# Joining the delta rule's inverse from diagonal 64-wide blocks, each in its own quarter of the TensorE array

## The chip, the core and the metric

The kernel runs on one core of a Trainium2 chip. The metric is device time in microseconds (us) of one execution. The work is two layers of a hybrid trunk (Hyena long convolution, gated delta rule, latent attention, mixture of experts) over 256 latent and 256 context tokens, in one program for all five engines.

## The reference, cut to what matters

The change lies in the gated delta rule. For each chunk of 64 tokens, head and direction the reference solves a unit lower triangular system of 64 rows and applies the inverse to the values and keys:

```python
C = GDN_CHUNK                                   # 64
gamma = jnp.exp(jnp.where(causal, gc[..., :, None] - gc[..., None, :], -jnp.inf))
kb = kc * bc[..., None]
m = jnp.where(strict, jnp.einsum('nbhid,nbhjd->nbhij', kb, kc) * gamma, 0.0)
eye = jnp.eye(C, dtype=F32)
t_inv = lax.linalg.triangular_solve(eye + m, jnp.broadcast_to(eye, m.shape), left_side=True, lower=True, unit_diagonal=True)
u = t_inv @ (vc * bc[..., None])
w = t_inv @ (kb * jnp.exp(gc)[..., None])
```

Then a scan over the chunks carries a 128 x 128 state per head and direction. It is done for context and latent tokens, 4 heads, both directions, in each of 2 layers.

## The kernel before, in words

The kernel works on chunks of 128 tokens in place of the reference's 64, so its inverse is one of 128 x 128 matrices. `gdn_pair` (L930) runs once per layer and pair of heads: it makes the features, then calls `gdn_system` (L1044) twice, for `base` 2 (the context) and `base` 0 (the latent tokens), and runs `gdn_scan` (L1202) for each. So there are 2 layers x 2 pairs x 2 bases = 8 systems. A system holds 8 matrices (2 directions, 2 chunks, 2 heads), four side by side in one tile of 128 x 512 for each direction `d`.

Inside a system, VectorE first inverts the diagonal 16-wide blocks by elimination (the loop over `j`, 15 steps of small operations; its rows are the ones that read `rsel` products). T holds the inverses and U their transposes. Then the blocks are joined: 16 to 32 wide, 32 to 64 wide (the two inner steps, the loop over `n` at L1148), and 64 to 128 wide (a step of its own behind it, already in 64 x 64 pieces). One inner step does, for each direction: N.U, four matmuls of 128 x 128 into one PSUM bank; `copy_predicated` on VectorE, which takes the wanted blocks of the bank into V (V starts as the identity); then T.V and V.T, four matmuls each into two banks, and two copies on ScalarE back into U and T. That is 3 bank products x 2 directions x 2 steps = 12 bank products a system, 96 in the program. Matrices that are block diagonal with blocks of 64 stay so until the last step.

The matmuls are in 32-bit floats; each of them is two MATMUL records in the trace (rows called `128*128 128x128 f32` are rows x columns of the stationary operand, then the shape that streams). The large projections are instead three matmuls on operands split into high and low parts, one record each (`128x512` and `128x256`).

The order of the work is made when the program is built. `Plan` (L227) gives every instruction an estimated cost by its engine and size, among them the matmul's by its output columns and stationary width, and keeps a clock for each engine. `run` (L544) goes through the layer's list of items (projections, splits of weights, merges); after each piece of an item, `tick` (L490) lets the streams go on (`gdn_system`, `gdn_scan`, `hyena`, `attend`, `filters`) whose inputs the plan takes to be ready by then, the delta rule's with priority. Every engine then executes its own list in that order, so a changed cost moves instructions of the whole program. The second pair of heads starts when the first has ended (`SERIAL`), and the merges of a layer need both pairs. `filters(l + 1)` is started by an item ahead of the last merge of layer 0 (`FILT`).

Every engine instruction is recorded under the line of one helper, L210, so the trace is read by operation and shape. `pg` is a page of SBUF, `bank` a bank of PSUM, `cst` the constants.

Of the kernel before, what the change touches and what calls it, by code (L numbers as in the profile page):

```python
# [360 lines left out]
class Trunk:  # L361
# [682 lines left out]
    def gdn_system(self, l, hp, base, fm, tm, sys):  # L1044
# [5 lines left out]
        nc = self.nc  # L1050
        v, g_, t_ = nc.vector, nc.gpsimd, nc.tensor
# [8 lines left out]
        u4 = lambda x: x.rearrange("p (u x) -> p u x", u=4)  # L1060
        m4 = lambda m: m[:, None, :].to_broadcast([128, 4, 128])
# [18 lines left out]
        N = M.get(2)  # L1080
# [17 lines left out]
        B = [M.get(2), M.get(2)]  # L1098
# [4 lines left out]
        for q in range(4):  # L1103
            b = self.bank()
# [12 lines left out]
        for j in range(14, -1, -1):  # L1117
            n = 16 - j
# [10 lines left out]
        T, U = [M.get(), M.get()], [M.get(), M.get()]  # L1129
# [3 lines left out]
        V = {}  # L1133
# [4 lines left out]
        for d in range(2):  # L1138
            yield self.plan.when(T[d].f())
            b = self.bank()  # L1140
# [3 lines left out]
            self.unbank(b)  # L1144
        X16.free()

        lm = self.c("lm").rearrange("p (n x) -> p n x", n=2).bitcast(U32)
        for i, n in enumerate((16, 32)):  # L1148
            for d in range(2):
                yield self.plan.when(U[d].f())  # L1150
                b = self.bank()
                for u in range(4):
                    t_.matmul(b[:, 128 * u:128 * u + 128], N.f(128, 512 * d + 128 * u), U[d].f(128, 128 * u), start=True, stop=True)
                v.copy_predicated(u4(V[n, d].f()), m4(lm[:, i]), u4(b))
                self.unbank(b)
            for d in range(2):
                yield self.plan.when(V[n, d].f())
                b, b2 = self.bank(), self.bank()
                for u in range(4):
                    t_.matmul(b[:, 128 * u:128 * u + 128], T[d].f(128, 128 * u), V[n, d].f(128, 128 * u), start=True, stop=True)  # L1160
                for u in range(4):
                    t_.matmul(b2[:, 128 * u:128 * u + 128], V[n, d].f(128, 128 * u), T[d].f(128, 128 * u), start=True, stop=True)
                nc.scalar.copy(U[d].f(), b)
                nc.scalar.copy(T[d].f(), b2)
                self.unbank(b)
                self.unbank(b2)
                V.pop((n, d)).free()

        yield
        b = self.bank()  # L1170
# [7 lines left out]
        b, b2 = self.bank(), self.bank()  # L1178
# [1384 lines left out]
```

## Time and profile before

| | before |
|---|---|
| time, median of 3 runs | 2144.14 us (2143.21 to 2147.01) |
| the profiled execution | 2145.01 us |
| its span | 2143.0 us |
| mean granted TensorE clock | 0.945 of full speed |
| PE busy (matmul) | 1919.7 us, 90% |
| VectorE busy | 1274.2 us, 59% |
| ScalarE busy | 869.3 us, 41% |
| GpSimd busy | 340.8 us, 16% |
| DMA | 403.62 MB, mean 188 GB/s |

The span is what lies between the first and the last recorded instruction; 2.0 us of the execution lie outside it. PE's busy time is the union of its matmul records, whose ends are modelled; PE works through a list of its own, so where it has a gap, it waited for another engine. The layers stand one after the other: the mixers of layer 0 up to about 740 us, its merge and routing, its experts from 900 to 1200, the mixers of layer 1 from 1250 to about 1750, and its experts from about 1835 to 2105.

### The profile page before, as it was taken

What the parts mean: (1) busy time and instruction counts of PE and PEld (TensorE: products, weight loads), DVE (VectorE), ACT (ScalarE), POOL (GpSimd) and SP (SyncE); (2) the same over time, 40 slices, a digit from 0 to 9 for tenths busy, and PEclk for the clock granted to TensorE, in tenths of its full rate; (3) what the DMA queues carried; (4) which work ended last, traced back from release to release, by engine and by line L of the source; (5) the groups of instructions that cost most, each with busy time, mean ns of one, the idle gap of its engine ahead of it and who ended that gap; (6) DMA issues with size and microseconds to landing.
All of it is one profiled execution on the core that took longest, in us unless ns stands there. A gap on an engine that the chain in (4) does not pass through costs nothing. (4 is left out here: it accounts for less than half of the span.)

```text
span 2143.0 us, 31289 instructions
## 1 busy us (share of the span) xinstructions
PE 1919.7 (90%) x11901; PEld 1434.8 (67%) x11902; DVE 1274.2 (59%) x2487; ACT 869.3 (41%) x1443; POOL 340.8 (16%) x318
## 2 busy tenths in 40 slices
PE   4999999999999898799999399988999987899993
PEld 1777887877778586688777277887787976433330
DVE  3656657555466646899888676666766666311113
ACT  3442334444433323388777444433454442010101
POOL 1211122000133003411100201221011212110002
PEclk9899999999999799899999799999999998899996
DMA  9735223312533156799997567422223448899971
GB/s 330 223 96 182 60 58 94 89 50 79 158 99 85 58 180 223 256 361 382 377 358 248 173 205 234 126 55 75 79 60 109 119 138 331 294 383 389 382 269 67
DMA packets 295751, 403.62 MB, mean 188 GB/s; under 512 B 43956, under 2 KB 185786, under 8 KB 295464
## 3 DMA queue, kind: packets, MB, share of 16 engines
q1 hardware_dynamic: 271512, 360.38, 50.4%
q10 hardware_dynamic: 13040, 21.33, 2.8%
q0 software_dynamic: 11040, 19.81, 2.7%
q8 instruction: 96, 1.57, 0.3%
q14 instruction: 63, 0.52, 0.1%
HBM read 394.56 MB, written 23.20 MB: 195 GB/s over the span
## 5 line engine op out<-in xcount | busy, mean ns | idle before, releaser
L210 PE MATMUL bank<-pg,pg 128*128 128x512 f32 (+5 forms) x9958 | 1701.7, 407 | 44.3 <-DVE pg L210 23.4
L210 PEld LDWEIGHTS bank<-pg,pg 128*128 128x128 f32 (+3 forms) x9958 | 1247.5, 172 | 445.9 <-issue 204.4
L210 DVE TENSOR_TENSOR pg<-pg,pg 128x1024 fp32r<-128x1024 f32 (+10 forms) x696 | 606.1, 901 | 217.7 <-ACT pg L210 206.9
L210 ACT CAST pg<-pg 128x1024 fp32r<-128x1024 f32 (+3 forms) x460 | 428.9, 965 | 260.9 <-DVE pg L210 167.4
L210 ACT COPY pg<-bank 128x512 f32<-128x512 f32 (+4 forms) x382 | 185.0, 506 | 368.2 <-PE bank L210 335.3
L210 PE MATMUL bank<-cst,pg 128*128 128x128 f32 (+3 forms) x935 | 145.0, 292 | 90.7 <-DVE pg L210 51.9
L210 PEld LDWEIGHTS bank<-cst,pg 128*128 128x128 f32 (+1 forms) x935 | 118.8, 160 | 149.5 <-issue 54.1
L210 POOL TENSOR_TENSOR pg<-pg,pg 128x1024 f32<-128x1024 f32 (+3 forms) x77 | 133.0, 1731 | 474.8 <-DVE pg L210 243.7
L210 ACT ACTIVATE pg<-bank 128x512 f32<-128x512 f32 (+1 forms) x116 | 60.9, 534 | 201.3 <-PE bank L210 195.5
L210 POOL DMA_INDIRECT yd<-pg,t_vi x28 | 28.2, 1006 | 481.5 <-ACT pg L210 246.0
L210 DVE SCALAR_TENSOR_TENSOR pg<-pg,bank 128x512 f32<-128x512 f32 (+1 forms) x92 | 54.1, 601 | 83.1 <-ACT pg L210 72.7
L210 DVE SCALAR_TENSOR_TENSOR pg<-bank,vec,pg 128x510 f32<-128x510 f32 (+3 forms) x112 | 75.4, 676 | 44.6 <-ACT pg L210 42.6
L210 ACT ACTIVATE pg<-pg 128x512 f32<-128x512 f32 (+4 forms) x71 | 50.0, 710 | 126.9 <-DVE pg L210 101.4
L210 DVE TENSOR_TENSOR pg<-bank,pg 128x512 fp32r<-128x512 f32 (+4 forms) x120 | 69.7, 597 | 52.0 <-ACT pg L210 36.3
L210 POOL TENSOR_TENSOR pg<-pg 128x512 f32<-128x512 f32 (+1 forms) x18 | 18.5, 1032 | 440.9 <-ACT pg L210 272.7
L210 DVE COPY pg<-bank 128x512 f32<-128x512 f32 x24 | 16.6, 692 | 105.5 <-PE bank L210 92.7
L210 DVE TENSOR_TENSOR pg<-pg,bank 128x512 f32<-128x512 f32 (+1 forms) x44 | 27.0, 613 | 76.0 <-PE bank L210 74.2
L210 ACT ACTIVATE pg<-bank,vec 128x512 f32<-128x512 f32 (+3 forms) x64 | 42.1, 658 | 58.8 <-PE bank L210 53.7
L210 ACT ACTIVATE pg<-bank,t_amx,t_asq 128x512 f32<-128x512 f32 (+1 forms) x48 | 33.9, 707 | 78.8 <-DVE t_amx L210 78.8
L210 ACT CAST pg<-bank 128x512 fp32r<-128x512 f32 (+1 forms) x72 | 35.7, 520 | 73.9 <-PE bank L210 69.1
L210 PE MATMUL bank<-pg,sc 128*32 128x512 f32 x384 | 54.7, 628 | 0.9 <-DMA pg<-in_w_ada_dram 0.9
L210 DVE TENSOR_REDUCE pg<-pg 128x128 f32<-128x1024 f32 (+15 forms) x128 | 42.9, 335 | 4.4
(250 smaller groups left out, 826.9 us busy)
## 6 DMA issues: line engine op xcount, KB each, us to landing
pg<-in_moe_w_dram SPq DMA_DIRECT2D x384, 512.0 KB
pg<-in_w_in_dram SPq DMA_DIRECT2D x120, 512.0 KB
pg<-in_w_ada_dram SPq DMA_DIRECT2D x96, 512.0 KB
pg<-in_w_out_dram SPq DMA_DIRECT2D x24, 512.0 KB
pg<-modd ACTq DMA_DIRECT2D x12, 512.0 KB
pg<-yd SPq DMA_DIRECT2D x12, 512.0 KB
pg<-in_mla_w_uq_dram SPq DMA_DIRECT2D x16, 288.0 KB
pg<-gcd POOLq DMA_DIRECT2D x16, 256.0 KB, 3.9
```

The lines of the kernel that those rows point to most:

```text
L210: return f(*a, **k)
```

## The change

The two inner steps no longer multiply 128 x 128 matrices, but only their diagonal 64-wide blocks. A helper `prod` does, for each of the four matrices, two matmuls of 64 x 64: one on partitions 0 to 63 that writes partitions 0 to 63 of the bank, one on partitions 64 to 127 that writes partitions 64 to 127. Each lies in its own quarter of the array; both write the same bank. The off-diagonal blocks of a bank are not written any more, so what reads it is cut in two as well: each `copy_predicated` of 128 x 512 becomes two of 64 x 4 x 64, each copy on ScalarE of 128 x 512 becomes two of 64 x 4 x 64.

```diff
+        halves = (0, 64)
+        quad = lambda x, o: u4(x)[o:o + 64, :, o:o + 64]
+
+        def prod(b, A, a0, B, b0):
+            for u in range(4):
+                for o in halves:
+                    t_.matmul(b[o:o + 64, 128 * u + o:128 * u + o + 64], A.f(64, a0 + 128 * u + o)[o:o + 64], B.f(64, b0 + 128 * u + o)[o:o + 64], start=True, stop=True)
         for i, n in enumerate((16, 32)):
             for d in range(2):
                 yield self.plan.when(U[d].f())
                 b = self.bank()
-                for u in range(4):
-                    t_.matmul(b[:, 128 * u:128 * u + 128], N.f(128, 512 * d + 128 * u), U[d].f(128, 128 * u), start=True, stop=True)
-                v.copy_predicated(u4(V[n, d].f()), m4(lm[:, i]), u4(b))
+                prod(b, N, 512 * d, U[d], 0)
+                for o in halves:
+                    v.copy_predicated(quad(V[n, d].f(), o), m4(lm[:, i])[o:o + 64, :, o:o + 64], quad(b, o))
                 self.unbank(b)
             for d in range(2):
                 yield self.plan.when(V[n, d].f())
                 b, b2 = self.bank(), self.bank()
-                for u in range(4):
-                    t_.matmul(b[:, 128 * u:128 * u + 128], T[d].f(128, 128 * u), V[n, d].f(128, 128 * u), start=True, stop=True)
-                for u in range(4):
-                    t_.matmul(b2[:, 128 * u:128 * u + 128], V[n, d].f(128, 128 * u), T[d].f(128, 128 * u), start=True, stop=True)
-                nc.scalar.copy(U[d].f(), b)
-                nc.scalar.copy(T[d].f(), b2)
+                prod(b, T[d], 0, V[n, d], 0)
+                prod(b2, V[n, d], 0, T[d], 0)
+                for o in halves:
+                    nc.scalar.copy(quad(U[d].f(), o), quad(b, o))
+                    nc.scalar.copy(quad(T[d].f(), o), quad(b2, o))
                 self.unbank(b)
                 self.unbank(b2)
                 V.pop((n, d)).free()
```

Since the plan takes a 64-wide matmul to be shorter, the order of the engines' lists changes from the first system on. Two places follow. In both, `64x64 x8` is one bank product of the change, `128x128 x4` one of before, and `128x512` or `32x512` is other work.

PE in layer 0, the first system of the program, before; `pg_180` is the page of U, `pg_181` that of the first step's V, `pg_96` and `pg_139` hold T of the two directions, `pg_138` is N, and the rows that write `bank_70` are a projection:

```order
L210 MATMUL bank_66<-pg_180_1446,pg_138_1081 128x128 x4
L210 MATMUL bank_68<-pg_180_1446,pg_138_1081 128x128 x4
L210 MATMUL bank_63<-pg_167_1318,sc 32x512 x2
L210 MATMUL bank_63<-pg_171_1395,sc 32x512 x2
L210 MATMUL bank_64<-cst_71,pg_162_1298 128x128 x4
L210 MATMUL bank_70<-pg_71_364,pg_173_1405 128x512 x2
L210 MATMUL bank_70<-pg_71_364,pg_174_1406 128x512
L210 MATMUL bank_70<-pg_72_372,pg_173_1405 128x512 x2
L210 MATMUL bank_70<-pg_72_372,pg_174_1406 128x512
L210 MATMUL bank_67<-pg_181_1449,pg_96_605 128x128 x4
L210 MATMUL bank_65<-pg_96_605,pg_181_1449 128x128 x4
L210 MATMUL bank_69<-pg_181_1449,pg_139_1090 128x128 x4
```

The same engine and place with the change, from the first step's last four products on (the projection writes `bank_64` here):

```order
L210 MATMUL bank_67<-pg_181_1449,pg_96_605 64x64 x8
L210 MATMUL bank_65<-pg_96_605,pg_181_1449 64x64 x8
L210 MATMUL bank_69<-pg_181_1449,pg_139_1090 64x64 x8
L210 MATMUL bank_66<-pg_139_1090,pg_181_1449 64x64 x8
L210 MATMUL bank_64<-pg_74_381,pg_173_1405 128x512 x2
L210 MATMUL bank_64<-pg_74_381,pg_174_1406 128x512
L210 MATMUL bank_64<-pg_75_390,pg_173_1405 128x512 x2
L210 MATMUL bank_64<-pg_75_390,pg_174_1406 128x512
L210 MATMUL bank_68<-pg_180_1446,pg_138_1081 64x64 x8
L210 MATMUL bank_70<-pg_180_1446,pg_138_1081 64x64 x8
```

Two pieces of the projection now stand between the first step's products and the second's, where before ten products followed one another; they were taken from what stood behind the system.

PE in layer 0, the last of its four systems, before: the end of the first inner step, the second one, and the projection behind them (`bank_68`).

```order
L210 MATMUL bank_63<-pg_473_5083,pg_469_4877 128x128 x4
L210 MATMUL bank_66<-pg_469_4877,pg_473_5083 128x128 x4
L210 MATMUL bank_64<-pg_380_3771,pg_466_4846 128x128 x4
L210 MATMUL bank_70<-pg_472_5079,pg_466_4846 128x128 x4
L210 MATMUL bank_69<-pg_473_5083,pg_366_3540 128x128 x4
L210 MATMUL bank_65<-pg_366_3540,pg_473_5083 128x128 x4
L210 MATMUL bank_67<-pg_474_5086,pg_469_4877 128x128 x4
L210 MATMUL bank_63<-pg_469_4877,pg_474_5086 128x128 x4
L210 MATMUL bank_68<-pg_77_400,pg_481_5114 128x512 x2
L210 MATMUL bank_68<-pg_77_400,pg_482_5115 128x512
```

The same place with the change: the end of the first inner step, and the start of what stands between it and the second. The rows that read `pg_494` and `pg_495` are the DFT of layer 1's Hyena filters.

```order
L210 MATMUL bank_63<-pg_500_5384,pg_498_5380 64x64 x8
L210 MATMUL bank_67<-pg_498_5380,pg_500_5384 64x64 x8
L210 MATMUL bank_64<-pg_500_5384,pg_498_5380 64x64 x8
L210 MATMUL bank_69<-pg_498_5380,pg_500_5384 64x64 x8
L210 MATMUL bank_66<-pg_502_5411,pg_494_5348 128x512 x2
L210 MATMUL bank_66<-pg_502_5411,pg_495_5349 128x512
L210 MATMUL bank_66<-pg_504_5442,pg_494_5348 128x512 x2
L210 MATMUL bank_66<-pg_504_5442,pg_495_5349 128x512
L210 MATMUL bank_68<-pg_503_5417,pg_494_5348 128x512 x2
L210 MATMUL bank_68<-pg_503_5417,pg_495_5349 128x512
```

All 48 matmuls of that DFT now stand inside the system, between its two inner steps; before, they stood behind the delta rule's end in this layer. The scan behind the system has lost the other work that stood between its products.

## Rows read from the trace of the kernel before

**Rows 1.** The page: PE, PEld, VectorE, ScalarE and GpSimd busy over the whole span.

```profile
PE 1919.7 (90%) x11901; PEld 1434.8 (67%) x11902; DVE 1274.2 (59%) x2487; ACT 869.3 (41%) x1443; POOL 340.8 (16%) x318
```

**Rows 2.** Windows: us, busy us of each engine (records), granted clock, DMA share, GB/s.

```profile
100.00:300.00 200.00, 196.01 (x1230) 158.37 (x1229) 125.42 (x253) 74.39 (x135) 38.26 (x43) 0.98 0.35 106
300.00:500.00 200.00, 197.77 (x981) 157.34 (x981) 120.01 (x281) 85.66 (x164) 14.15 (x11) 1.00 0.30 78
500.00:700.00 200.00, 196.89 (x1167) 156.61 (x1166) 117.64 (x262) 84.53 (x166) 43.37 (x44) 0.99 0.36 108
700.00:740.00 40.00, 29.80 (x111) 18.87 (x110) 26.92 (x65) 13.04 (x22) 4.07 (x4) 0.71 0.05 15
1355.00:1500.00 145.00, 128.09 (x949) 119.16 (x950) 93.39 (x234) 54.86 (x111) 28.57 (x32) 0.92 0.24 61
1600.00:1750.00 150.00, 131.75 (x1041) 123.00 (x1042) 94.48 (x221) 65.76 (x126) 29.93 (x33) 0.92 0.42 119
```

**Rows 3.** Waits of PE in 700 to 740 us, layer 0's end: total, times, longest.

```profile
PE bank L210 <- ACT pg L210: 5.0, 4, 2.3
PE bank L210 <- POOL pg L210: 4.9, 2, 4.6
```

**Rows 4.** Waits of PE in layer 1, 1355 to 1500 us and then 1600 to 1750 us.

```profile
PE bank L210 <- ACT pg L210: 9.0, 6, 3.1
PE bank L210 <- POOL pg L210: 5.8, 1, 5.8
PE bank L210 <- DVE pg L210: 4.8, 5, 2.9
...
PE bank L210 <- DVE pg L210: 12.1, 6, 4.6
PE bank L210 <- POOL pg L210: 8.0, 1, 8.0
```

**Rows 5.** Timeline of PE, merged runs: start us, us from first start to last end.

```profile
288.36 2.84 PE L210 MATMUL bank<-pg,pg 128*128 128x128 f32 x24
1530.13 3.16 PE L210 MATMUL bank<-pg,pg 128*128 128x512 f32 x13
299.96 1.03 PE L210 MATMUL bank<-pg,pg 64*64 64x64 f32 x15
299.06 2.83 PE L210 MATMUL bank<-pg,pg 128*128 128x512 f32 x22
```

**Rows 6.** PE by shape in 285 to 302 us: records | busy us, mean ns.

```profile
L210 PE MATMUL bank<-pg,pg 128*128 128x128 f32 x96 | 11.3, 276 | 0.4 <-DVE pg L210 0.4
L210 PE MATMUL bank<-pg,pg 128*128 128x512 f32 x17 | 4.7, 409 | 0.0
L210 PE MATMUL bank<-pg,pg 64*64 64x64 f32 x16 | 1.1, 221 | 0.0
```

**Rows 7.** Timeline of PE: 16 records in one quarter; then 8 and 8 in two.

```profile
299.85 1.14 PE L210 MATMUL bank<-pg,pg 64*64 64x64 f32 x16
302.51 0.96 PE L210 MATMUL bank<-pg,pg 64*64 64x64 f32 x16
```

**Rows 8.** PE by shape: 32-column pieces in 2000 to 2100 us, then lone ones.

```profile
L210 PE MATMUL bank<-pg,pg 128*32 128x512 f32 x872 | 95.4, 593 | 0.0
...
L210 PE MATMUL bank<-pg,pg 96*128 96x512 f32 x64 | 31.9, 622 | 0.0
```

**Rows 9.** VectorE by shape: the predicated copy, and two shapes of one operation.

```profile
L210 DVE COPY_PREDICATED pg<-cst,bank 128x512 f32<-128x512 uint32 x32 | 22.8, 730 | 22.7 <-PE bank L210 22.4 <-POOL pg L210 0.2
...
L210 DVE TENSOR_TENSOR pg<-bank,pg 128x512 f32<-128x512 f32 x16 | 10.7, 687 | 10.2 <-PE bank L210 9.0 <-issue 1.2
...
L210 DVE TENSOR_TENSOR pg<-bank,pg 128x256 f32<-128x256 f32 x16 | 6.4, 419 | 3.0 <-PE bank L210 3.0
```

**Rows 10.** ScalarE by shape: copies out of PSUM.

```profile
L210 ACT COPY pg<-bank 128x512 f32<-128x512 f32 x220 | 126.5, 587 | 299.5 <-PE bank L210 282.2 <-issue 8.0 <-DMA pg<-in_moe_w_dram 5.1
...
L210 ACT COPY pg<-bank 64x256 f32<-64x256 f32 x24 | 8.7, 365 | 10.8 <-PE bank L210 10.6
```

## The prediction

> **What bounds the kernel now.** I read the page first: PE is busy for 90% of the span, no other engine for more than 59% [rows 1]. That is an average, so I cut the span at the eight systems. The first pair of heads of layer 0 lies in 100 to 300 us, the second in 500 to 740, those of layer 1 in 1355 to 1500 and 1600 to 1750 [rows 2]. In the first three windows of layer 0 PE has 98% of the time, at a granted clock of 0.98 to 1.00: whatever PE is spared there, the next work takes at once. Layer 0's end differs: in 700 to 740 us PE is busy for 29.8 of 40 us, at a granted clock of 0.71, and waits for the delta rule's last steps on ScalarE and GpSimd [rows 2, 3]. In layer 1 PE is idle for 17 of 145 and 18 of 150 us [rows 2]; the longest single waits, 5.8 and 8.0 us, are for GpSimd at the ends of the two pairs' chains [rows 4]. So the sum has two parts: PE's work, which counts fully where PE is the bound, and what the chains let through elsewhere.
>
> **PE's work: the products.** Before, a bank product is 8 records of 128 x 128. A run of 24 lasts 2.84 us, its last record 0.276, so they start (2.84 - 0.276) / 23 = 0.112 us apart and a product costs 8 x 0.112 = 0.892 us (from the unrounded pace) [rows 5, 6]. Now it is 16 records of 64 x 64. Such records exist in the last joining step: 15 in one quarter last 1.03 us, so (1.03 - 0.221) / 14 = 0.058 us apart [rows 5, 6]. A quarter takes 8 of them, 0.464 us. Had the quarters to take turns, a product would cost 0.928 us, slightly more than before; the change lives on their running side by side.
>
> What do the rows say of that? The two visits in rows 7 have 16 records each. The first keeps to one quarter and lasts 1.14 us. In the second, 8 records lie in one quarter and the next 8 in another (same partitions read, other partitions written, other bank); it lasts 0.96 us, so the second eight began while the first eight ran, though they stand behind them in the list [rows 7]. The experts of layer 1 write four 32-column pieces side by side into one bank, each to its own partitions: 872 records take 95.4 us, 0.109 us each, where a lone record of the same 512 columns takes 31.9 / 64 = 0.498 [rows 8]. So column pieces overlap, in one bank too, and the list is read far enough ahead. Not shown is one thing: two quarters that read different partitions at once. The Trainium skill, "TensorEngine Tiling (Array Packing)", "Gotcha 1: PSUM Pressure", speaks against the change here: it says that different row tiles can't access one PSUM bank at the same time. By that rule the quarters would take turns; no row here shows it either way, and it is the first rival below.
>
> I take overlap, because the nearest rows (one bank, other partitions) overlap almost completely: 0.892 - 0.464 = 0.428 us for each of 96 products, **-41.1 us**. The other end is 0.928 - 0.892 = +0.036 each, +3.5 us.
>
> **PE's work: entering and leaving.** Changing between full and quarter shapes costs time. The run of 22 in rows 5 is three records of 512 columns, a visit of 16 small ones, and three again. Less the last record's 0.409 it has 21 steps in 2.42 us. At the paces of the runs alone, 0.23 for 512 columns ((3.16 - 0.409) / 12) and 0.058, five large and 16 small steps are 2.08, so a visit costs 0.34 us [rows 5, 6]. Most of the other 15 look alike. Counted in PE's list, there were 16 visits (two in a system); with the change there are 39, since other work stands between the products more often than not. 23 x 0.34 = **+7.8 us**. PE's work is thus 33.3 us less: 16.9 in layer 0 (8.3 in the first pair) and 16.4 in layer 1.
>
> **VectorE and ScalarE.** 32 predicated copies of 0.730 us become 64 of half the columns. Their price is not in the trace: no gain from fewer columns would be 0.730, half 0.365; the nearest pair of shapes, 512 against 256 columns of one operation, falls from 0.687 to 0.419 [rows 9], so I take 0.730 - 0.268 = 0.462. That is 64 x 0.462 - 32 x 0.730 = +6.2 us of VectorE (ends 0 and +23.4). 64 copies on ScalarE of 0.587 us become 128 of 0.365 [rows 10]: +9.1 us. Both engines have room (59% and 41%), so as work I cost this at nothing: PE's other matmuls in between cover it [rows 1]. If that cover is gone, a step's chain is longer by 0.19 us for the predicated copies of one direction and by 4 x 0.365 - 2 x 0.587 = 0.29 for its copies; two directions and two steps make 1.9 us a system. The last system of layer 1 has its 12 products in one stretch now, with no cover at all.
>
> **What the chains let through.** Pages, DMA issues and the experts' stages follow PE's list and move with it. In the first pair of layer 0, all 8.3 us pass through. In the second pair 8.6 are saved, but the filters' 48 matmuls, 48 x 0.23 = 11 us, now stand inside the last system. They delay the scan by that and are gone from behind it, which cancels; but the scan had 24 matmuls of 512 columns between its products, 5.5 us, which have been drawn forward, and so that much waiting is laid open beside the 10 us that PE waits there already [rows 2, 3]. I take 5 us back. In layer 1 PE's list reaches waits that GpSimd, VectorE and ScalarE end, 20 and 21 us in all in the two windows [rows 4]. A PE that arrives earlier waits longer, unless the chain ahead got shorter too; each system's products are part of that chain, so some of the 16.4 us does come through. Between all and nothing I take half, 8 us back. The sum: -41.1 + 7.8 + 5 + 8 = **-20.3 us**. The profiled execution took 2145.0 us, so 2124.7; it lies 0.9 us above the median of the runs, so I say 2124.0.
>
> **The rivals.**
> - *The quarters take turns.* Mechanism: different row groups, one bank. 96 x 0.036 + 7.8 = +11.3 us of PE work, time 2156. It decides as soon as a product costs over 0.892 - 7.8 / 96 = 0.81 us, that is when fewer than about 2 of its 16 steps overlap. For it: no row shows two row groups at once. Against it: rows 7 and 8. Chance 0.13; slower.
> - *The chains take it all.* The work leaves PE's list, but the second pairs' ends and layer 1 wait as before, with ScalarE's 1.9 us a system on top, and the waits lower the granted clock as in 700 to 740 us [rows 2]. Only the first pair's 8.3 us pass, less up to 8 x 1.9 = 15: 2136 to 2151. For it: rows 3 and 4. Against it: three of layer 0's windows are full of PE work. Chance 0.20: 0.08 faster, 0.08 within 0.2%, 0.04 slower.
> - *All of it passes.* The waits in layer 1 are behind the systems' own products, and a shorter system brings everything behind it forward, the waits too: -33.3 us or a little more where the new order is luckier, 2111. Against it: rows 3 and 4 show waits of other engines' making. Chance 0.17; faster.
>
> **How the numbers follow.** The forecast, that overlap holds and a part passes, 2114 to 2134 us, has 0.50 and is the likeliest; I predict 2124.0. The range of 8 in 10 reaches down to 2108, past the third rival's 2111 for a luckier order, and up to 2146, into the second rival; outside are the first rival and tails. 0.2% is 4.3 us, about what a measurement of this kernel can tell from no change. Faster by more than that: 0.50 + 0.17 + 0.08 = 0.75; within: 0.08; slower: 0.13 + 0.04 = 0.17.
>
> **What would show it.** Right: in a run of 64 x 64 records alone, 16 to a product, the records start 0.03 us apart on average, not 0.058; 768 records of 128 x 128 are gone and 1536 of 64 x 64 have come; PE's busy time is some 30 us less, not 41; the predicated copies take about 0.46 us, ScalarE's 0.365; layer 0's first window-and-a-half is 8 us shorter; PE's waits in layer 1 grow by some 8 us. Wrong: small records 0.058 us apart (the quarters take turns); a visit that costs much more than 0.34 us now that two quarters drain; waits for VectorE and ScalarE between the products; or an end of layer 0 that comes no earlier.

## Result: slower by 1.6%, with the products as fast as forecast

The changed kernel takes **2179.36 us** (median of 4 runs, 2177.05 to 2184.15), the kernel before, timed beside it, 2143.68: a ratio of 1.0161, 95% interval 1.0145 to 1.0176. The forecast was 2124.0 us, its range ended at 2146. It is wrong in sign.

Read the profile after against the one before. The page's first part comes first, in the same columns as [rows 1]:

```profile
PE 1914.9 (88%) x12669; PEld 1416.4 (65%) x12670; DVE 1280.9 (59%) x2519; ACT 876.6 (40%) x1507; POOL 339.6 (16%) x318
```

PE is busy for only 4.8 us less, in a span that is 39.5 us longer (2182.5 against 2143.0). Has the change failed to make the products cheaper? The groups by shape (records | busy us, mean ns) say no; they answer to [rows 6, 9, 10]:

```profile
L210 PE MATMUL bank<-pg,pg 64*64 64x64 f32 x1792 | 76.3, 232 | 11.1 <-ACT pg L210 9.1 <-DVE pg L210 1.8
L210 DVE COPY_PREDICATED pg<-cst,bank 64x256 f32<-64x256 uint32 x64 | 28.3, 443 | 19.3 <-PE bank L210 17.9
L210 ACT COPY pg<-bank 64x256 f32<-64x256 f32 x152 | 50.4, 366 | 46.9 <-PE bank L210 44.0 <-ACT pg L210 1.0
```

And the timeline of PE (start us, us of a merged run), which answers to [rows 5, 7]:

```profile
193.08 1.15 PE L210 MATMUL bank<-pg,pg 64*64 64x64 f32 x32
...
197.18 2.02 PE L210 MATMUL bank<-pg,pg 64*64 64x64 f32 x62
```

Two products, 32 records, take 1.15 us; less the last record's 0.232 the records start (1.15 - 0.232) / 31 = 0.030 us apart, and in the longer run (2.02 - 0.232) / 61 = 0.029. One quarter alone starts them 0.058 apart [rows 5], so the two quarters run side by side.

The loss is found by cutting both spans at the same pieces of work: from the first `rsel` product of a layer to its router (us start:end, length, busy of PE, PEld, VectorE, ScalarE and GpSimd with records, granted clock, DMA share, GB/s). First before, then after; in each, layer 0 and layer 1:

```profile
157.30:844.10 686.80, 659.69 (x3584) 525.54 (x3582) 410.27 (x863) 268.36 (x490) 104.00 (x94) 0.97 0.36 108
...
1319.80:1804.80 485.00, 437.98 (x3140) 391.07 (x3140) 314.13 (x723) 201.36 (x392) 75.90 (x80) 0.94 0.40 117
```

```profile
155.60:859.00 703.40, 649.81 (x3967) 511.98 (x3967) 413.93 (x882) 270.92 (x522) 104.54 (x94) 0.95 0.35 105
...
1339.60:1841.90 502.30, 437.44 (x3524) 384.88 (x3524) 315.90 (x733) 206.10 (x424) 73.23 (x79) 0.90 0.39 113
```

These stretches are longer by 16.6 and 17.3 us; another 5.2 lie in the stretch ahead of layer 1's. Inside them PE is idle for 53.6 us where it was 27.1, and for 64.9 where it was 47.0. In layer 1 its busy time has fallen by only 0.5 us, at a granted clock of 0.90 in place of 0.94 (means over the stretch). The waits of PE in layer 0's stretch, before and then after (total, times, longest), show who ended the idle time:

```profile
PE bank L210 <- ACT pg L210: 12.0, 10, 2.5
PE bank L210 <- DVE pg L210: 9.8, 12, 4.1
PE bank L210 <- POOL pg L210: 4.9, 2, 4.6
```

```profile
PE bank L210 <- ACT pg L210: 30.5, 18, 10.4
PE bank L210 <- DVE pg L210: 13.3, 15, 3.5
PE bank L210 <- POOL pg L210: 9.3, 2, 9.0
```

The longest is at the second matmul of the filters (`t_fw`), in front of the last system's products. Timeline of PE after; then, of VectorE, one shape in 687.8 to 694.7 us, and the row of the timeline that follows:

```profile
687.16 0.64 PE L210 MATMUL bank<-pg,t_fw 33*64 33x256 f32 x2
698.17 1.11 PE L210 MATMUL bank<-pg,t_fw 64*64 64x256 f32 x2 [10.36 <-ACT pg L210]
```

```profile
L210 DVE TENSOR_TENSOR pg<-pg,pg 128x1024 fp32r<-128x1024 f32 x3 | 3.6, 1218 | 0.0
...
694.75 0.53 DVE L210 TENSOR_SCALAR pg<-bank,t_fv 64x256 f32<-64x256 f32 x1
```

PE's bank is ready at 687.8, but VectorE reads it at 694.75, since three subtractions of 128 x 1024 (the splits of weights into high and low parts, 3.6 us) and small steps of the last system's elimination come first in its list. ScalarE waits for VectorE, PE for ScalarE, and behind that one matmul in PE's list stand the system's products. Nothing in this chain belongs to the change. That made the first question: are the instructions at fault or their order?

### The profile page after: what moved, and what is told of

Its sections match the earlier page's. It is cut to its first block, busy times and chain, and to the rows that moved or that the text cites. A ratio compares the mean times of both kernels' runs of the same rounds, so it can differ in the third digit from the quotient of the medians.

```text
span 2182.5 us, 32947 instructions
## 1 busy us (share of the span) xinstructions
PE 1914.9 (88%) x12669; PEld 1416.4 (65%) x12670; DVE 1280.9 (59%) x2519; ACT 876.6 (40%) x1507; POOL 339.6 (16%) x318
## 5 line engine op out<-in xcount | busy, mean ns | idle before, releaser
L210 PE MATMUL bank<-pg,pg 128*128 128x512 f32 (+7 forms) x10738 | 1691.7, 394 | 68.0 <-ACT pg L210 33.8
L210 PEld LDWEIGHTS bank<-pg,pg 128*128 128x128 f32 (+4 forms) x10738 | 1227.8, 169 | 481.0 <-issue 211.2
L210 DVE TENSOR_TENSOR pg<-pg,pg 128x1024 fp32r<-128x1024 f32 (+13 forms) x696 | 604.6, 898 | 218.9 <-ACT pg L210 207.4
L210 ACT COPY pg<-bank 64x256 f32<-64x256 f32 (+5 forms) x446 | 190.3, 455 | 393.0 <-PE bank L210 353.8
L210 POOL TENSOR_TENSOR pg<-pg,pg 128x512 f32<-128x512 f32 (+3 forms) x76 | 130.5, 1722 | 469.6 <-DVE pg L210 239.6
L210 POOL DMA_INDIRECT yd<-pg,t_vi x28 | 28.3, 1010 | 481.3 <-ACT pg L210 250.5
L210 DVE COPY pg<-bank 128x512 f32<-128x512 f32 x24 | 16.6, 692 | 105.6 <-PE bank L210 83.8
L210 DVE TENSOR_TENSOR pg<-bank,cst 32x256 f32<-32x256 f32 (+1 forms) x56 | 28.5, 518 | 44.3 <-PE bank L210 33.2
```

The source lines that it names most:

```text
L210: return f(*a, **k)
```

## Experiments

All of them use two small tools. `told` gives an instruction to the plan, which prices it and advances its clocks, without issuing it; `plan.off` hides the instructions that are issued. So the plan can write the lists for one set of prices while the program holds other instructions. The plan's prices, for a bank product: 855 ns before, 427 with the change; for the predicated copies of a bank 602 and 672; for ScalarE's 478 and 529 (the text of `e6` below has 427 for 478). `plan.force` sets a price by hand. Each run is compared with the kernel before, run on the same chip (its medians there: 2141.6 to 2144.2 us).

**Instructions and order apart.** `e1_old_order` has the change's instructions and tells the plan the old ones, so every engine's list keeps the old order, with the old pages and banks:

```diff
+        def told(eng, op, *a, **k):
+            self.plan.enter(eng, op, a, k)
         def prod(b, A, a0, B, b0):
             for u in range(4):
+                told("tensor", "matmul", b[:, 128 * u:128 * u + 128], A.f(128, a0 + 128 * u), B.f(128, b0 + 128 * u), **full)
+            self.plan.off = True
+            for u in range(4):
...
+            self.plan.off = False
```

and so for the copies. 

> The change's instructions in the order of before: the plan is told the old 128-wide matmuls and full copies, and the quarter matmuls and half copies are issued in their place. Theory 'order' (the quarters do what was forecast, and the 35 us are lost by the new order of the engines' lists): PE's work falls by 96 x 0.428 = 41.1 us less 20 more visits x 0.34 = 6.8, so between 2110 us (all passes) and 2130 (a part waits). Rival 'instructions' (the half copies, the visits or a lower clock cost the time in any order): 2165 to 2180, near the change.

`e2_new_order_alone` is the reverse: before's instructions, told the change's. 

> The instructions of before in the order of the change: the plan is told the quarter matmuls and half copies, the 128-wide matmuls and full copies are issued. Theory 'order': the order alone costs what the change lost plus what its PE work saved where PE is the bound, so 2190 to 2215 us. Rival 'instructions': 2144, as before.

`e4_old_order_layer1` tells the old ones in layer 1 only (`if l == 1`). 

> The change with the plan told the old costs in layer 1 only; layer 0 keeps the order of the change. Theory 'order', the losses of the two layers independent: layer 0 ends 15 us late as in the change, layer 1 loses its 22 us and gains up to its 16 us of PE work, so 2135 to 2155 us. Rival 'instructions': 2175 to 2180. Rival 'all from layer 0': the same 2175 to 2180, told from the former by the time between the two layers' marks.

`e3_filters_later` is the change with one setting moved:

```diff
-FILT = 'gategdn1'
+FILT = 'gategdn2'
```

> The change, with the next layer's filters started one item later (at gate 2 of the last merge in place of gate 1), so that they stand behind the delta rule's end in layer 0 and not inside its last system. Theory 'order, the filters in layer 0': the 10.4 us that PE waited at the filters' second matmul in front of the last system's products go, and routing in layer 0 comes some 15 us earlier, so 2160 to 2167 us. Rival (the delta rule's chain is as long without them, and PE waits elsewhere): 2175 to 2180.

| run | instructions | order | us | ratio to before |
|---|---|---|---|---|
| change | new | new | 2179.36 | 1.0161 [1.0145, 1.0176] |
| e1_old_order | new | old | 2129.74 | 0.9931 [0.9913, 0.9948] |
| e2_new_order_alone | old | new | 2190.04 | 1.0223 [1.0206, 1.0240] |
| e4_old_order_layer1 | new | new in layer 0 | 2159.55 | 1.0078 [1.0062, 1.0095] |
| e3_filters_later | new | new, filters later | 2169.22 | 1.0135 [1.0103, 1.0167] |

`e1` and `e2` lie at the edges of the ranges that "order" had given them; `e4` and `e3` lie above theirs, `e4` by 4.6 us and `e3` by 2.2, and no run lies in a rival's range. The two parts stand alone: the instructions gain 13 to 15 us in the old order (and 11 to 13 in the new: e2 to the change), by the medians and by the ratios, and the order by itself costs 47. Some 30 us of that come from layer 0's order (e1 to e4) and 18 to 20 from layer 1's. "Order" takes in the pages and banks that each value gets, since the plan hands them out as it goes; no run separates the two. Letting the filters go later gives back 6 to 10 of the 36, at the edge of the intervals. The same two stretches in e1:

```profile
156.10:829.30 673.20, 642.76 (x3966) 505.64 (x3965) 413.42 (x878) 270.95 (x522) 103.69 (x94) 0.97 0.37 110
...
1307.60:1787.60 480.00, 426.65 (x3525) 375.77 (x3525) 316.18 (x734) 205.44 (x424) 75.31 (x79) 0.94 0.40 120
```

Compare with the change, record for record the same work: 642.8 against 649.8 us busy in layer 0 (clock 0.97 and 0.95), 426.7 against 437.4 in layer 1 (0.94 and 0.90). So of the 53.8 us between the two spans, 23.2 + 11.5 are more idle time of PE, and 7.0 + 10.8 are the same records at a lower granted clock. The wait at the filters is 2.3 us in e1, and other matmuls stand between the two of the filters.

**Are the new prices wrong, or is any other price bad?** The plan's new prices are too low beside the trace (a product 0.427 against 0.464 us and a share of a visit; a half copy 0.336 against 0.443). If that drew work forward for chains believed too short, true prices would mend it. `e5_told_paces` tells the measured ones:

```diff
+            self.plan.force = 116
...
+                self.plan.force = 440
...
+                self.plan.force = 365
```

> The change's instructions; the plan is told the paces that the trace of the change shows (a bank product 4 x 116 = 464 ns, a predicated half copy 440 ns, a ScalarE half copy 365 ns) where the change lets it take 427, 336 and 264 ns. The new order of the lists has been shown to be what costs the change its time. Theory A, the plan's prices for the new instructions are too low, so that it draws work forward for chains that it thinks shorter than they are: with true prices most of the 50 us between the change and its instructions in the old order come back, 2125 to 2145 us. Theory B, the old order was a lucky or chosen one and any other order of the same planner costs tens of us, whatever the prices: 2150 to 2190 us.

`e6_told_copies_only` tells the old products and the new copies. 

> The change's instructions; the plan is told the old price of the products (855 ns) and, as in the change, the two half copies (672 instead of 602 ns for a predicated pair, 529 instead of 427 ns for a pair on ScalarE). Theory A, the low price of the products makes the bad order: prices of the chain that are a little higher than in the old order do no harm, 2122 to 2140 us. Theory B, any other order costs tens of us: 2150 to 2185 us.

`p1_before_repriced` is before with `self.plan.force = 192` for its own matmuls, priced at 214. 

> Before's instructions, all of them; the plan alone is told 192 instead of 214 ns for each of a product's four matmuls (10% less), and so writes another order of the lists. Nothing of the change is in it. Theory A, what harms is a price far from the truth: a tenth off the products of the inverse, which are 86 of some 1900 us of PE's work, moves the time by under 10 us, 2134 to 2152. Theory B, any other order than the old one costs tens of us: 2153 to 2190 us.

`e5` took 2185.71 us (1.0193 [1.0171, 1.0215]), `e6` 2153.70 (1.0048 [1.0030, 1.0066]), `p1` 2169.06 (1.0128 [1.0111, 1.0144]). Theory A, the low prices, falls: true prices are no better than the plan's. A price a tenth lower costs a kernel with no new instruction 27 us. So I asked how small a shift is enough, in both directions: before again, told 210, 217 and 222.

`q1_before_210`: 

> Before's instructions; the plan is told 210 instead of 214 ns for each of a product's four matmuls (2% less). A tenth less has cost 27 us. Theory B1, the old order is one picked out: the settings beside the planner were chosen for these very prices, and any other price, in either direction, writes an order that is slower, 2148 to 2180 us. Theory B2, orders scatter by tens of us around a middle and the old one is an ordinary draw: the three small shifts of this job fall on both sides of 2143 us, 2115 to 2170. Theory B3, the loss grows with the shift: 2% costs a fifth of what 10% cost, 2143 to 2150 us.

`q2_before_217`: 

> Before's instructions; the plan is told 217 instead of 214 ns (1.5% more). B1, picked out: 2148 to 2180 us. B2, ordinary draw: on either side, 2115 to 2170 us. B3, in proportion, and a price above the truth is the safe side: 2138 to 2146 us.

`q4_before_222`: 

> Before's instructions; the plan is told 222 instead of 214 ns (4% more; 223 is what a quarter of a product takes in the trace). B1, picked out: 2148 to 2180 us. B2, ordinary draw: on either side, 2115 to 2170 us. B3, in proportion: 2138 to 2152 us.

| told, ns a matmul | 192 | 210 | 214 (before) | 217 | 222 |
|---|---|---|---|---|---|
| us | 2169.06 | 2151.63 | 2144.16 | 2154.59 | 2168.06 |
| ratio to before | 1.0128 | 1.0037 | 1 | 1.0046 | 1.0105 |

The intervals of 210 and 217 are 1.0023 to 1.0051 and 1.0031 to 1.0061. B2, the ordinary draw, fell: no shift gained. The three times lie in B1's range, and all three outside B3's: the loss grows with the shift, but not in proportion, and upwards too, where B3 had it safe. The old order is a dip at just these prices.

**Which piece of the order.** `h1` and `h2` are e4 with the new prices in one pair of layer 0 only (`old = l == 1 or hp == 0`, and `hp == 1`).

`h1_new_prices_second_pair`: 

> The change's instructions; the plan is told the old prices everywhere but in the second pair of heads of layer 0. The old order everywhere gave 2129.7 us, the new order in both pairs of layer 0 2159.6. Here PE's list is the old one up to the second pair, and the filters' matmuls stand ahead of the last system. Theory F, the filters and what is drawn forward with them empty the stretch behind the last system: nearly all of the 30 us, 2150 to 2162 us. Theory G, each piece of disorder costs its share: 2138 to 2149 us.

`h2_new_prices_first_pair`: 

> The change's instructions; the plan is told the old prices everywhere but in the first pair of heads of layer 0. The filters stand where they stood before. F: little is lost, 2127 to 2138 us. G, each piece of disorder costs its share: 2139 to 2152 us.

`r4` and `r1` are before at its own prices with `FILT = 'gategdn0'` and `'gategdn2'`.

`r4_before_filters_earlier`: 

> Before, at its own prices; the second layer's filters are let go one step earlier, so that their 48 matmuls stand ahead of or inside the last system of layer 0, as in the change. F: PE meets GpSimd's wait at the end of the last system without them, 9 instead of 4.6 us, and waits in front of them; 2152 to 2165 us. If their place is of no weight: 2139 to 2148 us.

`r1_before_filters_later`: 

> Before, at its own prices; the second layer's filters are let go one step later. If the old setting is the best at the old prices (picked out): 2148 to 2165 us. If it is an ordinary one: 2132 to 2147 us.

`h1` took 2153.10 us (1.0043 [1.0029, 1.0057]), `h2` 2138.79 (0.9980 [0.9963, 0.9997]): beside e1 the second pair's prices cost about 23 us and the first's 9 (G had shares near equal, F nothing in the first pair; it lies between). Not all of the 23 lie where the prices were changed: beside e1, h1's stretch in layer 0 is 20.4 us longer (693.6 for 673.2) and its stretch in layer 1 8.9 (488.9 for 480.0), because the redraw reaches on into layer 1's last system. h1 has the same waits as the change, 10.4 us at the filters and 9.0 for GpSimd. But `r4` took 2145.00 (1.0017 [1.0001, 1.0033]), although GpSimd's wait is as long there:

```profile
745.12 0.69 PE L210 MATMUL bank<-cst,pg 128*128 128x128 f32 x2 [10.12 <-POOL pg L210]
```

So GpSimd's 10 us don't explain the loss by themselves. The filters' place in front of the last system is not tested by `r4`: unlike what its expectation says, they stand behind that system's products there (from 703 us on no record of 64 x 64 is left in layer 0), and the wait at them is 3.6 us. `e3` tests it: it has no filters in front of the last system, yet PE waits there for VectorE:

```profile
702.25 1.97 PE L210 MATMUL bank<-cst,pg 128*128 128x128 f32 x8 [8.77 <-DVE pg L210]
```

So F as I had put it falls. `r1` took 2151.79 (1.0041 [1.0028, 1.0053]): at the old prices the old setting is better than its neighbour, while with the change's prices the neighbour is no worse (e3).

What most of the slower orders share shows in the time from a system's `rsel` products, which feed its elimination on VectorE, to the transposes behind the elimination (`cst`). Timeline of PE at layer 0's last system, before and then after:

```profile
655.60 3.74 PE L210 MATMUL bank<-pg,rsel 128*128 128x128 f32 x32
675.62 1.04 PE L210 MATMUL bank<-cst,pg 128*128 128x128 f32 x8
...
669.77 3.74 PE L210 MATMUL bank<-pg,rsel 128*128 128x128 f32 x32
700.65 1.97 PE L210 MATMUL bank<-cst,pg 128*128 128x128 f32 x8 [1.38 <-DVE pg L210]
```

From start to start, 20.0 us have become 30.9. In between, VectorE's list has no split of 128 x 1024 before, and six of them (8.9 us) after. e1 and r4 have 20.0 us here too, h1 30.8, and e3 26.2 with five splits. At layer 1's last system it is 22.4 us before and 22.5 in e1, but 34.8 after, and 31.5 to 32.7 in q1, q4, r1 and h1. The lists of q1 are those of before up to layer 1's second pair, and from that pair's first `rsel` product to the router it takes 214.3 us for 203.4; VectorE's list has five splits in the last system's elimination for three. So splits that the plan lets into an elimination fit most of the loss at these two places. No run moved them alone, so this is read from traces and not shown by an experiment.

**A version that beats both.** The change halves a copy where the off-diagonal blocks need not be kept out: the predicated copy's mask is zero there, and of T[0] and U[1] only the diagonal blocks are read later. `e9` is e1 with these copies whole:

```diff
-                for o in halves:
-                    v.copy_predicated(quad(V[n, d].f(), o), m4(lm[:, i])[o:o + 64, :, o:o + 64], quad(b, o))
+                v.copy_predicated(u4(V[n, d].f()), m4(lm[:, i]), u4(b))
...
+                for x, y, whole in ((U[d], b, d == 1), (T[d], b2, d == 0)):
+                    if whole:
+                        nc.scalar.copy(x.f(), y)
```

`e9_old_order_fewer_copies`: 

> The change's instructions in the old order, but one predicated copy over all of a bank in place of two halves (its mask is zero outside the diagonal blocks), and one ScalarE copy of the whole bank for T[0] and U[1], of which only the diagonal blocks are read later. Removes 32 predicated halves at a net 2 x 0.442 - 0.730 = 0.15 us and 32 ScalarE pairs at a net 0.73 - 0.587 = 0.14 us from the chains, 1.2 us of a system's chain at most, 9 us over eight systems. If the chains' copies set the pace where PE waits, 2120 to 2127 us; if they lie beside other work, 2127 to 2131, as the change in the old order.

It took 2120.74 us (0.9904 [0.9887, 0.9920]), 1.0% faster than before and, by the two ratios, 0.27% or 6 us faster than e1; the two intervals overlap at their ends, so the step from e1 is likely and not shown. VectorE's row shows the whole copies:

```profile
L210 DVE COPY_PREDICATED pg<-cst,bank 128x512 f32<-128x512 uint32 x32 | 22.1, 723 | 10.9 <-PE bank L210 6.4 <-ACT pg L210 4.3
```

The same instructions in the order that the plan writes for them itself:

`e10_fewer_copies_own_order`: 

> The kernel with the change and the fewer copies, in the order that the plan writes for it when nothing is told: the version as one would write it. If the order is what decides (B1 or B2) it is slower than the same instructions in the old order, 2120.7 us, by tens of us: 2145 to 2180. If the fewer copies had taken the chain out of the bad order's waits, 2120 to 2140.

It took 2176.12 us (1.0136 [1.0111, 1.0161]). Two orders of the same instructions lie some 50 us apart by the ratios (55 by the medians, which come from two chips).

## Why the prediction was wrong

- **The quarters overlap: right.** 0.030 us a record was forecast, 0.029 to 0.030 measured. The Trainium skill, "TensorEngine Tiling (Array Packing)", "Gotcha 1: PSUM Pressure", says that two row tiles can't access one PSUM bank at the same time. By that rule the two quarters would take turns, and the 32 records would take about 31 x 0.058 + 0.232 = 2.0 us, an estimate from the pace of one quarter [rows 5]. They write one bank a product from two row groups and took 1.15 us; here the measurement decides.
- **PE's work, -33.3 us: right in size.** It is seen where the order is held, in e1. Layer 0's stretch has 659.7 - 642.8 = 16.9 us less work, at the same granted clock of 0.97; forecast 16.9. That it agrees to the tenth is luck: for the same records in the same order one execution differs from the next by 6 us (before 659.7, q1 653.5; e1 642.8, e9 637.2). Layer 1 has 11.3 less, forecast 16.4; what of the difference is clock and what visits is not separated. (e1 has 36 visits, the change 39; the 0.34 us of a visit was not measured again.)
- **The copies: right in duration, perhaps not quite free.** 0.443 us for 0.462, 0.366 for 0.365. "I cost this at nothing" may have been a little too good: e9 takes back 28.3 - 22.1 = 6.2 us on VectorE and 32 x (2 x 0.366 - 0.588) = 4.6 on ScalarE, and some 6 us seem to have come out as time.
- **What the chains let through, +13 us: right for the old order, and the failing step for the new one.** In e1 PE's idle time grows by 3.3 us in layer 0 (686.8 - 659.7 = 27.1 before, 673.2 - 642.8 = 30.4) and by 6.3 in layer 1, against 5 and 8. In all, the old order gave 13 to 15 of the 20.3 us: by these traces the two stretches are 18.6 us shorter, and 4.3 are lost outside them. But the changed kernel runs in another order, and there the step said: "Pages, DMA issues and the experts' stages follow PE's list and move with it." I had looked at the new lists in a few places and priced one, the last system of layer 0, at 5.5 us of uncovered scan. The order as a whole costs 47 us (e2), in both layers, and through other engines' lists as well as PE's: of the 26.5 us by which PE's idle time grew in layer 0, 18.5 are ended by ScalarE, and the longest wait is one that VectorE's list makes. I priced PE's list as if the others would always be ready for it.
- **The rivals.** "The quarters take turns" and "All of it passes" are out. "The chains take it all" named the right effects, ScalarE's waits and a lowered clock, but ended at 2151, because it took the waits of before as the worst case. Only the third rival allowed for a "luckier" order; no case allowed for an unluckier one, though nothing in the profile favoured one sign. The two measured parts add up to 2143.7 - 13 + 47 = 2178 us, against 2179.4.

That the old order sits at a dip is shown by the orders tried: the seven others in which before's own instructions ran (e2, p1, the three q, the two r) were all slower, by 0.2% (r4, whose interval begins at 1.0001) to 2.2%. That it was picked out on purpose at these prices is an inference from that.

## What to carry to other kernels

Where a planner orders the work by prices, a new instruction is two changes: what it costs, and a redrawn order of every list. Hold the order by telling the planner the old prices, and take both apart before judging either; here a shift of one price by 2% cost 0.4%, and true prices did not bring the old order's time back. In a prediction, give the redraw a term of its own, with its own spread on the slow side, and read the lists of all engines at the ends of the chains, not PE's alone.

## What was not expected of the hardware

In these runs PE's waits came with slower work. The same records of layer 1's stretch (3525, and 3524 seen) took 426.7 us of busy time at a granted clock of 0.94 (e1) and 437.4 at 0.90 (the change), where PE was idle for 64.9 in place of 53.3 us: 11.5 us of waiting came with 10.8 of slower work. The rate is not fixed: with the old products, e2 waits 15.3 us more than before in this stretch and works 5.7 us longer (443.7 of 506.0 us, clock 0.93). A busy total hides this: on the page PE's work seems to have shrunk by 4.8 us, and not by the 26.6 that e1's page shows:

```profile
PE 1893.1 (89%) x12669; PEld 1399.1 (66%) x12670; DVE 1281.6 (60%) x2519; ACT 876.3 (41%) x1507; POOL 340.4 (16%) x318
```
